# Output projections with the activations as the stationary operand, in a two-layer recurrent encoder

## The chip, the cores and the metric

The kernel runs on one core of one Trainium2 chip. The metric is the device time of one execution in microseconds (us); runs of one kernel are summed up by their median.

## What is computed

The reference is a trunk of two layers on 256 tokens of width 2048, all in float32. Each layer is a token mixer and a gated MLP, both behind an RMSNorm and both added to the residual; a last RMSNorm closes the trunk.

```python
for layer in range(2):
    hn = rmsnorm(h, norm_mix_g[layer])
    mix = mlstm_mixer(hn, ...) if layer == 0 else hgrn_mixer(hn, ...)      # each ends in  y @ w_out
    h = h + mix
    h = h + conv_glu(rmsnorm(h, norm_ffn_g[layer]), ...)                   # ends in  (gelu(c) * v) @ w_down
return rmsnorm(h, final_g)
```

The mixers are recurrences that run over the tokens in both directions: the mLSTM with 8 heads of width 256, HGRN2 with 16 heads of width 128. The MLP's hidden width is 5504, 43 tiles of 128. Four output projections add to the residual: `w_out` of the mLSTM, `w_down` of layer 0, `w_out` of HGRN2 and `w_down` of layer 1.

## The kernel before

All weights, some 440 MB, are streamed from memory once. Precision comes from a split: a float32 value is taken apart into a high part and a low part, and a product is computed from three terms, high by high, high by low and low by high. `split_weights` loads pieces of 2048 columns (`raw`, three buffers, on SP's queue), and makes two halves of 1024 columns each from it: ACT rounds `wh` out of `raw` (line 146), DVE subtracts to get `wl` (line 147), four buffers each. `stream` keeps three such halves ahead (LOOK) and issues the matmuls of a list of chunks in their order. An activation tile `x` for one k tile is 128 x 512: the 256 tokens of the high part, then the 256 of the low part.

There are two kinds of chunk. In an "fm" chunk (feature-major result) the weights are stationary and the tokens move. A chunk has 256 output features in two blocks f, and each k tile takes one pair of matmuls for each block:

```python
pe.matmul(ps[f], wh[:, c:c + P], x, start=st, stop=False)                          # line 197, 512 columns
pe.matmul(ps[f][:, 0:T], wl[:, c:c + P], x[:, 0:T], start=False, stop=sp)          # line 198, 256 columns
```

In a "tm" chunk (token-major result) a tile of `x` is stationary and 512 columns of the weights move, three matmuls for each half t of the tokens (lines 187 to 189). Before the change q, k of the mLSTM, q and both gates of HGRN2, both halves of the MLP and all output projections are fm; v and o of the mLSTM, v and g of HGRN2 are tm.

`Side` holds generators for small work, such as the heads of the mixers and the transposes of their results. `side.tick` advances a clock by an estimate of the matmul time after every k tile, and steps the generators that are due, so that their instructions land between the stream's matmuls in PE's queue. The framework orders each engine's instructions by a simulated timeline and may move them by a few places.

The residual `hx` is feature-major, 16 tiles `hT[k]` of 128 features by 256 tokens. `project` makes the chunks of an output projection: eight of them, 256 output features each. Its `done` adds the two column halves of a result to `hT[k]` (ACT copies one half to `b`, DVE adds twice, lines 310 to 312), and hands the tile to the `Norm` behind it. `Norm.add` scales the tile by the norm's weight and splits it into an `x` tile (`split`, lines 204 and 205), POOL squares it and sums the squares (lines 243 to 248), four small matmuls with a vector of ones sum over the features (L254, `pc`). `finish` takes the power -1/2 on POOL (line 280), and spreads it over the partitions by a diagonal matrix and a matmul (L286, `pr`). The scale itself is applied later, to the results of the next stage's matmuls.

The MLP runs in two parts of 22 and 21 hidden tiles: up chunks, down chunks, up chunks, down chunks. The very last chunk of the kernel has a form of its own (`last`, line 176): three matmuls of 256 columns for each k tile and block. After it the final norm is finished, DVE and POOL scale eight blocks (line 806), and eight transfers to the output follow on the queues of SP and ACT.

In the names of the trace `xt` is an x tile of a norm, `g` one of the MLP's hidden tiles, `ya` and `yb` the mixers' results, `mm` the accumulators of the stream, `pz` a transpose, `S` and `pn` matmuls of the mLSTM's heads (L426, L440), `pd` and `py` of HGRN2's (L616, L657, L658, L670), `Mb` rows of a running maximum that go through memory (`mscr`) on POOL's queue.

Of the kernel before, what the change touches and what calls it, by code (L numbers as in the profile page):

```python
# [30 lines left out]
    ("mix_g", 2 * KT), ("ffn_g", 2 * KT), ("a_head_g", KT), ("b_head_g", KT), ("final_g", KT),  # L31
# [13 lines left out]
MIX = 5  # L45
FIRST = (0, 1, 2, 4, 7, 10, 13, 16)
# [7 lines left out]
def trunk_kernel(ctx, tc, xT, pp_d, cst_d, w_first, w_aq, w_ak, w_av, w_ao, w_aout,  # L54
                 w_bq, w_bv, w_bg, w_bout, w_up, w_down, out, mscr, stop=9):
# [15 lines left out]
    hT = [hx[:, k] for k in range(KT)]  # L71
    ident = cst[:, C_ID:C_ID + P]
# [40 lines left out]
    class Chunk:  # L113
        def __init__(self, kind, src, nk, x, done, before=None, last=False):
            self.last = last
            self.kind, self.src, self.nk, self.x, self.done, self.before = kind, src, nk, x, done, before
            self.width = {"fm": 256, "tm": 512, "first": 512 + P}[kind]

    def split_weights(chunks):

        first = True
        for ch in chunks:
            total = ch.nk * ch.width
            cuts = [0]
            if ch.last and total % 1024:
                cuts.append(total % 1024)
# [24 lines left out]
    def stream(chunks):  # L151
# [10 lines left out]
        for ch in chunks:  # L162
# [4 lines left out]
            while k < ch.nk:  # L167
                fetch()
                wh, wl, n = ready.pop(0)
                if ch.last:  # L170
                    for f in range(2):
                        for kk in range(n):
                            x, c = ch.x(k + kk), kk * 256 + f * P
                            terms = ((wh, 0), (wl, 0), (wh, T))
                            for i, (w, o) in enumerate(terms):
                                pe.matmul(ps[f][:, 0:T], w[:, c:c + P], x[:, o:o + T], start=(k + kk == 0 and i == 0),  # L176
                                          stop=(k + kk == ch.nk - 1 and i == 2))
                    k += n
                    continue
                for kk in range(n):  # L180
# [13 lines left out]
                    else:  # L194
                        for f in range(len(ps)):
                            c = kk * ch.width + f * P
                            pe.matmul(ps[f], wh[:, c:c + P], x, start=st, stop=False)  # L197
                            pe.matmul(ps[f][:, 0:T], wl[:, c:c + P], x[:, 0:T], start=False, stop=sp)  # L198
                        side.tick(0.325 * len(ps))
# [23 lines left out]
    class Norm:  # L223
        def __init__(self, gname, goff, final=False, first=False):
            self.first = first
            self.g, self.o, self.final = gname, goff, final
            self.xs, self.pc = [], None

        def add(self, k):
            if self.final:  # L230
                if k % 2 == 0:
                    self.xs.append(keep.tile([P, 2, T], F32, tag=f"xt{k}", name=f"hg{k}"))
                act.activation(self.xs[k // 2][:, k % 2], hT[k], AF.Copy, scale=col(self.g, self.o + k))
            else:
                t = keep.tile([P, 2 * T], F32R, tag=f"xt{k}", name=f"xt{k}")
                split(t, hT[k], col(self.g, self.o + k))
                self.xs.append(t)
            if self.first:
                return
            eng = dve if k >= KT - 2 else pool  # L240
            if k == 0:
                self.acc = ev.tile([P, T], F32, tag="acc", bufs=2, name="acc")
                eng.tensor_tensor(self.acc, hT[k], hT[k], ALU.mult)  # L243
                return
            s = ev.tile([P, T], F32, tag="sq", bufs=2, name="sq")
            eng.tensor_tensor(s, hT[k], hT[k], ALU.mult)  # L246
            if k < KT - 2 or not self.final:
                eng.tensor_tensor(self.acc, self.acc, s, ALU.add)
                s = self.acc
            if k >= (KT - 3 if self.final else KT - 1):  # L250
                if self.pc is None:
                    self.pc = [aux("pc") for _ in range(2)]
                for t in range(2):
                    pe.matmul(self.pc[t][:, 0:1], s[:, t * P:(t + 1) * P], ones[:, 0:1],  # L254
                              start=(k == KT - 3 or not self.final), stop=(k == KT - 1))
            if k == KT - 1:
                self.finish()

        def squares(self, i, mp):
# [7 lines left out]
            if i == 3:  # L267
                a = self.acc4
                dve.tensor_tensor(a[:, 0:2 * T], a[:, 0:2 * T], a[:, 2 * T:4 * T], ALU.add)
                dve.tensor_tensor(a[:, 0:T], a[:, 0:T], a[:, T:2 * T], ALU.add)  # L270
                self.pc = [aux("pc") for _ in range(2)]
                for t in range(2):
                    pe.matmul(self.pc[t][:, 0:1], a[:, t * P:(t + 1) * P], ones[:, 0:1], start=True, stop=True)
                self.finish()

        def finish(self):
            self.rc = ev.tile([P, 2], F32, tag="rc", bufs=2, name="rc")
            for t in range(2):
                dve.tensor_scalar(self.rc[:, t:t + 1], self.pc[t][:, 0:1], 1.0 / D, EPS, ALU.mult, ALU.add)
            pool.tensor_tensor(self.rc, self.rc, hmx, ALU.pow)  # L280
            dg = ev.tile([P, T], F32, tag="sq", bufs=2, name="dg")
            for t in range(2):
                dve.tensor_scalar(dg[:, t * P:(t + 1) * P], ident, self.rc[:, t:t + 1], None, ALU.mult)
            self.pr = aux("pr")
            for t in range(2):
                pe.matmul(self.pr[:, t * P:(t + 1) * P], ones[:, 0:P], dg[:, t * P:(t + 1) * P], start=True, stop=True)  # L286
            self.R = ev.tile([P, T], F32, tag="R", bufs=2, name="R")
            act.copy(self.R, self.pr[:, 0:T])

        def x(self, k):  # L290
            return self.xs[k]

# [6 lines left out]
    def project(wsrc, nk, x, norm):  # L299

        def done(c):
            def f_(ps):
                for f in range(2):
                    k = 2 * c + f
                    if norm is not None and norm.final and c == 7:
                        dve.tensor_tensor(hT[k], hT[k], ps[f][:, 0:T], ALU.add)
                        norm.add(k)
                        continue
                    b = ev.tile([P, T], F32, tag="b", bufs=3, name="b")
                    act.copy(b, ps[f][:, T:2 * T])  # L310
                    dve.tensor_tensor(hT[k], hT[k], ps[f][:, 0:T], ALU.add)
                    dve.tensor_tensor(hT[k], hT[k], b, ALU.add)  # L312
                    if norm is not None:
                        norm.add(k)
            return f_
        return [Chunk("fm", wsrc(c), nk, x, done(c), last=(norm is not None and norm.final and c == 7))
                for c in range(8)]
# [6 lines left out]
    def mlstm(norm, nxt):  # L324
# [6 lines left out]
        def first_x(k):  # L331
            if k == len(norm.xs):
                norm.add(k)
# [86 lines left out]
        def head(st, j):  # L420
# [30 lines left out]
            for t in range(2):  # L451
                jk = ev.tile([P, T], F32, tag="jk", bufs=1, name="jk")
                act.activation(jk, y[:, t], AF.Square, accum_out=ss[:, t:t + 1])
# [22 lines left out]
        for pr in range(AH // 2):  # L476
# [34 lines left out]
            def done_first(ps, done_v=done_v):  # L511
                done_v(ps[0:2])
                gates(ps[2])

# [4 lines left out]
            chunks.append(Chunk("fm", w_aq[pr], KT, norm.x, done_q))  # L519
# [16 lines left out]
    def hgrn(norm, nxt):  # L536
# [59 lines left out]
        def head(hd):  # L596
# [75 lines left out]
            for t in range(2):  # L672
                jk = ev.tile([P, T], F32, tag="jk", bufs=1, name="jk")
# [63 lines left out]
    def ffn(layer, norm, nxt):  # L737
# [4 lines left out]
        def begin():  # L742
            box["mp"] = stack.enter_context(tc.tile_pool(name="ff", bufs=1))

# [20 lines left out]
        for part, (f0, nf) in enumerate(((0, FA), (FA, FB))):  # L765
            GT = []
            for i in range(nf):
                chunks.append(Chunk("fm", w_up[layer, f0 + i], KT, norm.x, done_up(f0 + i, i, GT),
                                    begin if f0 + i == 0 else None))
            chunks += project(lambda c: w_down[layer, c][:, f0 * 256:(f0 + nf) * 256], nf,  # L770
# [11 lines left out]
    n0, n1, n2, n3 = Norm("mix_g", 0, first=True), Norm("ffn_g", 0), Norm("mix_g", KT), Norm("ffn_g", KT)  # L782
    nf = Norm("final_g", 0, final=True)
    chunks = mlstm(n0, n1)
    if stop > 1:
        c, close0 = ffn(0, n1, n2)
        chunks += c
    if stop > 2:
        c = hgrn(n2, n3)
        b = c[0].before  # L790

        def swap():
            close0()
            b()
        c[0].before = swap
        chunks += c
    if stop > 3:
        c, close1 = ffn(1, n3, nf)
        chunks += c
    stream(chunks)  # L800
    side.drain()
    if stop > 3:
        order = ((0, pool), (2, dve), (3, dve), (1, pool), (4, dve), (5, dve), (6, dve), (7, dve))
        for n, (c, eng) in enumerate(order):
            r = (nf.R if eng is pool else nf.pr[:, 0:T]).unsqueeze(1).broadcast_to([P, 2, T])
            eng.tensor_tensor(nf.xs[c], nf.xs[c], r, ALU.mult)
            (nc.sync if n % 2 else nc.scalar).dma_start(out[c], nf.xs[c])
        close1()
    else:
        for c in range(KT // 2):  # L810
# [82 lines left out]
```

## Time and profile before

| | |
|---|---|
| median of 3 runs | 2452.22 us (2452.0 to 2452.59) |
| the profiled execution's own time | 2451.01 us |
| its span, first to last instruction | 2449.2 us |
| mean granted TensorE clock | 0.998 |
| PE busy | 2432.1 us, 99% |
| DVE busy | 1759.7 us, 72% |
| ACT busy | 1221.2 us, 50% |
| POOL busy | 267.4 us, 11% |
| weight pieces, time from issue to landing | 4.9 us for 1 MB |

Times in the profile count from the start of the span. The stages follow each other: the mLSTM's projections to 310 us, its output projection to 400, the first MLP to 1116 (down projections 645 to 767 and 1000 to 1116), HGRN2 to 1626, its output projection to 1719, the second MLP (down projections 1964 to 2086 and 2319 to 2436), the tail to 2449. The length of a matmul's record holds its way through the array, which overlaps the next matmul; the stream's rate is read from the distance between starts in the timeline. A row of the windows gives the stretch, its length, the busy time and instructions of PE, PEld, DVE, ACT and POOL, the granted clock, the share of the DMA engines and GB/s.

### The profile page before, as it was taken

What the parts mean: (1) busy time and instruction counts of PE and PEld (TensorE: products, weight loads), DVE (VectorE), ACT (ScalarE), POOL (GpSimd) and SP (SyncE); (2) the same over time, 40 slices, a digit from 0 to 9 for tenths busy, and PEclk for the clock granted to TensorE, in tenths of its full rate; (3) what the DMA queues carried; (4) which work ended last, traced back from release to release, by engine and by line L of the source; (5) the groups of instructions that cost most, each with busy time, mean ns of one, the idle gap of its engine ahead of it and who ended that gap; (6) DMA issues with size and microseconds to landing.
All of it is one profiled execution on the core that took longest, in us unless ns stands there. A gap on an engine that the chain in (4) does not pass through costs nothing.

```text
span 2449.2 us, 36986 instructions
## 1 busy us (share of the span) xinstructions
PE 2432.1 (99%) x14462; PEld 2108.3 (86%) x14462; DVE 1759.7 (72%) x2943; ACT 1221.2 (50%) x1890; POOL 267.4 (11%) x325
## 2 busy tenths in 40 slices
PE   9999999999999999999999999999999999999998
PEld 7888888888888888888888888888888888888887
DVE  7766577777656777668888888888777755677754
ACT  6655455444444444445455555545544444444443
POOL 0100032000000000122222222224000000000022
PEclk9999999999999999999999999999999999999999
DMA  7654555555556555555544445445555555555553
GB/s 261 189 179 160 184 187 184 191 191 191 179 189 202 189 189 189 181 183 191 172 160 168 162 165 172 160 156 201 186 191 191 186 189 194 189 189 189 185 190 125
DMA packets 65920, 448.88 MB, mean 183 GB/s; under 512 B 7616, under 2 KB 8256, under 8 KB 15568
## 3 DMA queue, kind: packets, MB, share of 16 engines
q1 hardware_dynamic: 63936, 443.03, 54.2%
q0 software_dynamic: 800, 2.16, 0.6%
q8 instruction: 113, 1.85, 0.3%
q10 hardware_dynamic: 1008, 1.32, 0.2%
q14 instruction: 63, 0.52, 0.1%
HBM read 444.32 MB, written 2.16 MB: 182 GB/s over the span
## 4 chain that ended last, share of the span: by engine, by line
PE 98%; DVE 1%; ACT 0%; issue 0%; DMA 0%; SPq 0%; POOL 0%; DVEq 0%; POOLq 0%
PE mm L197 53%; PE mm L198 26%; PE mm L187 5%; PE mm L189 5%; PE mm L188 5%; PE pd L616 1%; PE pn L440 1%; PE mm L176 1%; PE py L670 1%; DVE wl L147 0%; PE S L426 0%; PE pd L657 0%; DMA raw<-in_w_first 0%; DVE QK L629 0%; PE pz L691 0%
## 5 line engine op out<-in xcount | busy, mean ns | idle before, releaser
L147 DVE TENSOR_TENSOR wl<-raw,wh 128x1024 fp32r<-128x1024 f32 (+1 forms) x864 | 1047.5, 1214 | 546.4 <-ACT wh L146 533.5
L197 PE MATMUL mm<-xt,wh 128*128 128x512 f32 x3776 | 1319.5, 395 | 0.0
L146 ACT CAST wh<-raw 128x1024 fp32r<-128x1024 f32 (+1 forms) x864 | 884.1, 1025 | 833.2 <-PE mm L197 481.5
L198 PE MATMUL mm<-xt,wl 128*128 128x256 f32 x3776 | 1049.9, 278 | 0.0
L197 PEld LDWEIGHTS mm<-xt,wh 128*128 128x128 f32 x3776 | 708.3, 188 | 164.3
L198 PEld LDWEIGHTS mm<-xt,wl 128*128 128x128 f32 x3776 | 710.1, 188 | 0.8
L197 PE MATMUL mm<-g,wh 128*128 128x512 f32 x1334 | 462.6, 394 | 0.0
L198 PE MATMUL mm<-g,wl 128*128 128x256 f32 x1334 | 369.5, 277 | 0.0
L197 PEld LDWEIGHTS mm<-g,wh 128*128 128x128 f32 x1334 | 250.1, 188 | 58.0
L198 PEld LDWEIGHTS mm<-g,wl 128*128 128x128 f32 x1334 | 250.5, 188 | 0.0
L187 PE MATMUL mm<-wh,xt 128*128 128x512 f32 x512 | 201.9, 398 | 3.1 <-ACT xt L204 2.5
L188 PE MATMUL mm<-wl,xt 128*128 128x512 f32 x512 | 201.5, 394 | 0.4 <-DVE wl L147 0.4
L189 PE MATMUL mm<-wh,xt 128*128 128x512 f32 x512 | 200.6, 393 | 0.0
L209 ACT COPY b<-mm 128x256 f32<-128x256 f32 x237 | 87.6, 370 | 172.2 <-PE mm L198 172.2
L243 POOL TENSOR_TENSOR acc<-hx 128x256 f32<-128x256 f32 x4 | 4.8, 1203 | 1238.3 <-DVE hx L312 1238.3
L187 PEld LDWEIGHTS mm<-wh,xt 128*128 128x128 f32 x512 | 95.7, 188 | 23.3 <-ACT xt L204 2.7
L189 PEld LDWEIGHTS mm<-wh,xt 128*128 128x128 f32 x512 | 96.5, 188 | 19.9
L188 PEld LDWEIGHTS mm<-wl,xt 128*128 128x128 f32 x512 | 96.5, 188 | 19.4 <-DVE wl L147 0.8
L197 PE MATMUL mm<-yb,wh 128*128 128x512 f32 x256 | 89.6, 396 | 0.0
L197 PE MATMUL mm<-ya,wh 128*128 128x512 f32 x256 | 89.1, 394 | 0.0
L246 POOL TENSOR_TENSOR sq<-hx 128x256 f32<-128x256 f32 x52 | 62.7, 1214 | 193.4 <-DVE hx L312 191.2
L210 DVE TENSOR_TENSOR a<-mm,b 128x256 f32<-128x256 f32 x86 | 36.5, 425 | 50.9 <-ACT b L209 50.7
(188 smaller groups left out, 1999.2 us busy)
## 6 DMA issues: line engine op xcount, KB each, us to landing
raw<-in_w_up SPq DMA_DIRECT2D x172, 1024.0 KB, 4.9
raw<-in_w_down SPq DMA_DIRECT2D x64, 1024.0 KB, 4.8
raw<-in_w_bq SPq DMA_DIRECT2D x48, 1024.0 KB, 4.9
raw<-in_w_ao SPq DMA_DIRECT2D x16, 1024.0 KB, 4.9
raw<-in_w_aout SPq DMA_DIRECT2D x16, 1024.0 KB, 4.9
raw<-in_w_bv SPq DMA_DIRECT2D x16, 1024.0 KB, 4.9
raw<-in_w_bg SPq DMA_DIRECT2D x16, 1024.0 KB, 4.9
raw<-in_w_bout SPq DMA_DIRECT2D x16, 1024.0 KB, 4.9
```

The source lines that it names most:

```text
L146: act.copy(wh[:, :m], r)
L147: dve.tensor_tensor(wl[:, :m], r, wh[:, :m].bitcast(F32), ALU.subtract)
L176: pe.matmul(ps[f][:, 0:T], w[:, c:c + P], x[:, o:o + T], start=(k + kk == 0 and i == 0), stop=(k + kk == ch.nk - 1 and i == 2))
L187: pe.matmul(ps[t], xh, wh[:, c], start=st, stop=False)
L188: pe.matmul(ps[t], xh, wl[:, c], start=False, stop=False)
L189: pe.matmul(ps[t], xl, wh[:, c], start=False, stop=sp)
L197: pe.matmul(ps[f], wh[:, c:c + P], x, start=st, stop=False)
L198: pe.matmul(ps[f][:, 0:T], wl[:, c:c + P], x[:, 0:T], start=False, stop=sp)
L209: act.copy(b, ps[:, T:2 * T])
L210: dve.tensor_tensor(dst, ps[:, 0:T], b, ALU.add)
L246: eng.tensor_tensor(s, hT[k], hT[k], ALU.mult)
L440: pe.matmul(pn[:, 0:258], w, v, start=(i == 0), stop=(i == len(parts) - 1))
```

## The change

All output projections become tm: `project` makes four chunks of 512 output features, the weights' layout in memory changes from 256 to 512 columns, and the residual becomes token-major (`hm`, the same storage as `hx`, two halves t of 128 tokens by 2048 features). Two new loads on POOL's queue bring x in that layout behind the first chunk. `done` adds 512 columns for each t straight from PSUM.

`Norm.add` becomes a square with a sum along the row on ACT, and a generator `turn`, which transposes the residual in groups of four on PE and splits the tiles straight out of PSUM; after the last chunk it finishes the norm. `FinalNorm` takes the place of the last norm: it stays token-major, multiplies by `final_g` (loaded and spread over the partitions when the second MLP begins) and scales rows. The last chunk issues all matmuls of the remaining pieces for t = 0, then `half`, then the same for t = 1.

In an fm chunk `side.tick` moves from behind the pair to between the two matmuls of the second block's pair. Chunks have a new parameter `turns`: so many transposes of the identity into an unused accumulator, inside the second block's first pair. q chunks of the mLSTM's head pairs get 0, 1, 2 and 1, the first up chunk of each second part 1 (layer 0) and 2 (layer 1). A tile of 192 bytes (`lead`) is put ahead of the MLP's tiles. `final_g` leaves the packed parameters `pp`, which lose 64 bytes a partition.

```diff
+LEAD = 48
+    hm = hx.rearrange("p k t -> p (k t)").rearrange("p (a c) -> p a c", a=2)
...
-                if ch.last:
-                    for f in range(2):
-                        for kk in range(n):
-                            x, c = ch.x(k + kk), kk * 256 + f * P
-                            terms = ((wh, 0), (wl, 0), (wh, T))
...
+                if ch.last and k + sum(p[2] for p in ready) + n == ch.nk:
+                    pieces_, k0 = [(wh, wl, n)] + ready, k
+                    for t in range(2):
+                        k = k0
+                        for wh, wl, n in pieces_:
+                            for kk in range(n):
+                                x, c = ch.x(k), slice(kk * 512, (kk + 1) * 512)
+                                xh, xl = x[:, t * P:(t + 1) * P], x[:, T + t * P:T + (t + 1) * P]
+                                pe.matmul(ps[t], xh, wh[:, c], start=False, stop=False)
+                                pe.matmul(ps[t], xh, wl[:, c], start=False, stop=False)
+                                pe.matmul(ps[t], xl, wh[:, c], start=False, stop=k == ch.nk - 1)
+                                k += 1
+                        ch.half(ps[t], t)
+                    return
...
                             pe.matmul(ps[f], wh[:, c:c + P], x, start=st, stop=False)
+                            if f and k == 0 and ch.turns:
+                                it = aux("turns")
+                                for i in range(ch.turns):
+                                    pe.transpose(it[:, i * P:(i + 1) * P], ident, ident)
+                            if f:
+                                side.tick(0.325 * len(ps))
                             pe.matmul(ps[f][:, 0:T], wl[:, c:c + P], x[:, 0:T], start=False, stop=sp)
-                        side.tick(0.325 * len(ps))
...
+        def add(self, c):
+            if c == 0:
+                self.ss = ev.tile([P, 2, 4], F32, tag="ss8", bufs=2, name="ss8")
+            cs = slice(512 * c, 512 * c + 512)
             for t in range(2):
+                square(hm[:, t, cs], self.ss[:, t, c:c + 1])
+            side.push(self.turn(c))
+
+        def turn(self, c):
+            yield 2.5
+            for k0 in (4 * c, 4 * c + 2):
+                pz = aux("pz")
+                for k in (k0, k0 + 1):
+                    for t in range(2):
+                        o = (k - k0) * T + t * P
+                        pe.transpose(pz[:, o:o + P], hm[:, t, k * P:(k + 1) * P], ident)
+                for k in (k0, k0 + 1):
+                    self.take(k, pz[:, (k - k0) * T:(k - k0 + 1) * T])
+                yield 1.0
+            if c == 3:
...
+                self.finish([ss[:, t, 0:1] for t in range(2)])
...
+    class FinalNorm:
...
+        def half(self, ps, t):
+            side.drain()
+            cs = slice(D - 512, D)
+            h = hm[:, t, cs]
+            dve.tensor_tensor(h, h, ps, ALU.add)
+            square(h, self.ss[:, t, 3:4])
+            last = self.mp.tile([P, 512], F32, tag="fl", bufs=2, name="fl")
+            dve.tensor_tensor(last, h, self.g[:, cs], ALU.mult)
+            rc = self.rc[:, t:t + 1]
+            dve.tensor_scalar(rc, self.ss[:, t, 3:4], 1.0 / D, rc, ALU.mult, ALU.add)
+            pool.tensor_tensor(rc, rc, hmx[:, 0:1], ALU.pow)
+            for c in range(4):
+                v = last if c == 3 else hm[:, t, 512 * c:512 * c + 512]
+                if c % 2:
+                    act.activation(v, v, AF.Copy, scale=rc)
+                else:
+                    dve.tensor_scalar(v, v, rc, None, ALU.mult)
+                (nc.scalar if c % 2 else nc.sync).dma_start(out[t, :, 512 * c:512 * c + 512], v)
...
         def done(c):
             def f_(ps):
...
+                for t in range(2):
+                    h = hm[:, t, 512 * c:512 * c + 512]
+                    dve.tensor_tensor(h, h, ps[t], ALU.add)
+                if norm is not None:
+                    norm.add(c)
             return f_
...
+        chunks = [Chunk("tm", wsrc(c), nk, x, done(c)) for c in range(4)]
...
                 gates(ps[2])
+                for t in range(2):
+                    pool.dma_start(hm[:, t], x_d[t])
...
-            chunks.append(Chunk("fm", w_aq[pr], KT, norm.x, done_q))
+            chunks.append(Chunk("fm", w_aq[pr], KT, norm.x, done_q, turns=(0, 1, 2, 1)[pr]))
...
+            box["mp"].tile([P, LEAD], F32, name="lead")
+            if isinstance(nxt, FinalNorm):
+                nxt.begin(box["mp"])
...
+                                    turns=(2 if layer else 1) if part and i == 0 else 0))
```

More of the change, by code (lines that the diff above doesn't have):

```diff
@@ L113, in trunk_kernel, with __init__ @@
     class Chunk:
-        def __init__(self, kind, src, nk, x, done, before=None, last=False):
-            self.last = last
+        def __init__(self, kind, src, nk, x, done, before=None, last=False, turns=0):
+            self.last, self.turns = last, turns
             self.kind, self.src, self.nk, self.x, self.done, self.before = kind, src, nk, x, done, before
@@ L223, in trunk_kernel, with __init__, take @@
     class Norm:
[L224 to L257, printed above, removed]
+        def __init__(self, gname, goff):
+            self.g, self.o = gname, goff
+            self.xs, self.done = [None] * KT, False
+        def take(self, k, src):
+            self.xs[k] = keep.tile([P, 2 * T], F32R, tag=f"xt{k}", name=f"xt{k}")
+            split(self.xs[k], src, col(self.g, self.o + k))
         def squares(self, i, mp):
@@ L270, in squares @@
                 dve.tensor_tensor(a[:, 0:T], a[:, 0:T], a[:, T:2 * T], ALU.add)
-                self.pc = [aux("pc") for _ in range(2)]
+                pc = [aux("pc") for _ in range(2)]
                 for t in range(2):
[L273 to L277, printed above, removed]
-            for t in range(2):
-                dve.tensor_scalar(self.rc[:, t:t + 1], self.pc[t][:, 0:1], 1.0 / D, EPS, ALU.mult, ALU.add)
-            pool.tensor_tensor(self.rc, self.rc, hmx, ALU.pow)
-            dg = ev.tile([P, T], F32, tag="sq", bufs=2, name="dg")
+                    pe.matmul(pc[t][:, 0:1], a[:, t * P:(t + 1) * P], ones[:, 0:1], start=True, stop=True)
@@ L302, in f_ @@
             def f_(ps):
[L303 to L314, printed above, removed]
-            return f_
-        return [Chunk("fm", wsrc(c), nk, x, done(c), last=(norm is not None and norm.final and c == 7))
-                for c in range(8)]
+                for t in range(2):
+                    h = hm[:, t, 512 * c:512 * c + 512]
+                    dve.tensor_tensor(h, h, ps[t], ALU.add)
+                if norm is not None:
+                    norm.add(c)
+            return f_
+        chunks = [Chunk("tm", wsrc(c), nk, x, done(c)) for c in range(4)]
+        if isinstance(norm, FinalNorm):
+            chunks[3].last, chunks[3].half = True, norm.half
+        return chunks
     def slot(j, name, more=None):
@@ L513, in done_first @@
                 gates(ps[2])
+                for t in range(2):
+                    pool.dma_start(hm[:, t], x_d[t])
             if pr == 0:
@@ L781, in trunk_kernel, with swap @@
         pe.matmul(idle[:, 0:P], ones[:, 0:P], ones[:, 0:P], start=True, stop=True)
-    n0, n1, n2, n3 = Norm("mix_g", 0, first=True), Norm("ffn_g", 0), Norm("mix_g", KT), Norm("ffn_g", KT)
-    nf = Norm("final_g", 0, final=True)
+    n0, n1, n2, n3 = Norm("mix_g", 0), Norm("ffn_g", 0), Norm("mix_g", KT), Norm("ffn_g", KT)
+    nf = FinalNorm()
     chunks = mlstm(n0, n1)
[L785 to L799, printed above, removed]
-    stream(chunks)
[L801 to L810, printed above, removed]
-            nc.sync.dma_start(out[c], hx[:, 2 * c:2 * c + 2])
-        if stop == 2:
-            close0()
+    c, close0 = ffn(0, n1, n2)
+    chunks += c
+    c = hgrn(n2, n3)
+    b = c[0].before
+    def swap():
+        close0()
+        b()
+    c[0].before = swap
+    chunks += c
+    c, close1 = ffn(1, n3, nf)
+    chunks += c
+    stream(chunks)
+    close1()
 def _cols(w, width):
```

98 lines of the change are left out of this document (69 added, 29 removed).

## The prediction

> **What bounds the kernel now.** First the page: busy shares, and the chain that ended last.
>
> ```profile
> PE 2432.1 (99%) x14462; PEld 2108.3 (86%) x14462; DVE 1759.7 (72%) x2943; ACT 1221.2 (50%) x1890; POOL 267.4 (11%) x325
> ...
> PE 98%; DVE 1%; ACT 0%; issue 0%; DMA 0%; SPq 0%; POOL 0%; DVEq 0%; POOLq 0%
> ```
>
> PE is the chain from start to end. The timeline of PE shows no gap over 0.3 us in any stage but four places: the start, two of some 0.6 us at 15 to 17 us, 1.5 us at 1165 us, and the tail. So an edit is worth what it takes off PE's queue, or off the tail. Second, the windows by stage, here the first down projection and the tail after the last weight matmul:
>
> ```profile
> 644.90:766.90 122.00, 122.00 (x706) 106.70 (x705) 65.45 (x85) 52.11 (x67) 0.00 (x0) 1.00 0.57 188
> ...
> 2436.10:2449.20 13.10, 1.81 (x14) 1.46 (x12) 5.33 (x12) 0.88 (x2) 3.19 (x3) 0.69 0.43 160
> ```
>
> The clock is granted in full, DVE is busy for half of a projection. A matmul's record (395 ns) is a latency; what counts is the distance between starts. Third, the timeline of PE in three streams: fm pairs in q of head pair 1, fm pairs in an up chunk, tm matmuls in o.
>
> ```profile
> 113.26 0.40 PE L197 MATMUL mm<-xt,wh 128*128 128x512 f32 x1
> ...
> 114.32 0.40 PE L197 MATMUL mm<-xt,wh 128*128 128x512 f32 x1
> ```
> ```profile
> 524.24 0.39 PE L197 MATMUL mm<-xt,wh 128*128 128x512 f32 x1
> ...
> 525.27 0.40 PE L197 MATMUL mm<-xt,wh 128*128 128x512 f32 x1
> ```
> ```profile
> 175.37 0.39 PE L187 MATMUL mm<-wh,xt 128*128 128x512 f32 x1
> ...
> 176.05 0.39 PE L187 MATMUL mm<-wh,xt 128*128 128x512 f32 x1
> ```
>
> Each fence but the last spans three pairs: 1.06 us (353 ns a pair, "slow") and 1.03 (346.7 over long stretches, "fast"). The last spans three 512-column matmuls: 0.68 us, 226.7 each. Fm knows only these two rates: up and down chunks and output projections run fast from 324 to 1150 us and from 1664 to 2420, while q and k of mLSTM and most of HGRN are slow. A fm chunk entered from a tm chunk starts slow in nearly every case. It goes on slow until something is put between, and what that is matters: after any group of transposes or of norm matmuls (L254, L286, L468, L691) it was fast; after py or pd groups standing between pairs it stayed slow. Every group of two or four that landed inside a pair, between its wh and its wl matmul, was followed by the fast rate:
>
> ```profile
> 1269.65 0.40 PE L197 MATMUL mm<-xt,wh 128*128 128x512 f32 x1
> 1269.89 0.38 PE L691 MATMUL pz<-cst,y 128*128 128x128 f32 x2
> 1270.03 0.36 PE L198 MATMUL mm<-xt,wl 128*128 128x256 f32 x1
> 1270.23 0.40 PE L197 MATMUL mm<-xt,wh 128*128 128x512 f32 x1
> ```
>
> **The change part by part.** The profiled execution took 2451.01 us, its span is 2449.2; the median of the three runs is 2452.22, 1.2 above it. I sum against the span and carry the difference over to the median.
>
> *Projections as tm.* Removed: 1334 pairs on g, 256 on ya, 256 on yb, 1846 x 346.7 ns = 640.0 us, and the 126 L176 matmuls of the last chunk, 120 ns apart, 15.1. Added: 4 chunks x (16 + 16 + 2 x 43) k tiles = 472 steps of six 512-column matmuls, 472 x 6 x 226.7 ns = 642.0. All on PE: **-13.1**. Some 50 pairs of the two output projections now run slow: -0.3. The six new entries (the first six matmuls of a tm chunk cost some 30 ns together, the first fm pairs run slow until the first group): +0.4.
>
> *Transposes of the residual.* Each of three norms gets 32 transposes in groups of four. The nearest row is L468, the same form in a tm stream:
>
> ```profile
> 173.32 0.39 PE L189 MATMUL mm<-wh,xt 128*128 128x512 f32 x1
> 173.55 0.60 PE L468 MATMUL pz<-cst,y 128*128 128x128 f32 x4
> 173.91 0.48 PE L187 MATMUL mm<-wh,xt 128*128 128x512 f32 x1
> 174.23 0.39 PE L188 MATMUL mm<-wl,xt 128*128 128x512 f32 x1
> ```
>
> The group moves the next start by 0.36, the matmul behind it takes 0.32 instead of 0.227: 0.46 us. 24 groups: **+11.0** (+8.6 if the 0.1 behind it falls away). Four L254 groups go (0.45 each in streams, 0.4 in the last): -1.8. In one place the Trainium skill speaks against this part: its page "TensorE: Matmul & The Clock Gate", section "Part 4: PE-mode transpose", puts a transpose at about 275 ns in a kernel, bound by SBUF access. The records of L468 do last 272 ns, but their starts are 108 ns apart; by the page 96 x 275 ns would be an estimated 26 us.
>
> *Waits that the transposes bring.* PE is in order, so a group whose residual isn't added yet stops the weight stream. After a chunk's last matmul: 0.4 us to DVE's start, two adds of 512 from PSUM at 0.69 (L806's row), ready at 1.8 us; the groups come at the first tick past 2.5. DVE's weight subtraction (1.24 us) could stand ahead: then 3.1 against some 2.7. But PE lags the weights by four wh buffers, some 11 us, so it rarely does. Taken: 0; bound +0.4 x 12 chunks = +5. Behind each add in DVE's queue stand only later weight pieces, with that lead. Evacuation gets cheaper (copies and half the adds go; POOL's 1.2 us squares go), off the path: 0.
>
> *Side work and turns inside pairs.* In HGRN 530 pairs run slow, some 110 of them before the first group of a chunk. If the others turn fast: 420 x 6.6 ns = 2.8; py and pd inside a pair aren't in the trace, so bounds 0 and -2.8; taken **-2.3**, as every kind seen there turned it. The mLSTM q and k chunks of head pairs 1 to 3 (192 pairs) save 1.3. The seven added turns cost 0.13 (one) or 0.24 (two) by L691's groups: +0.9. Net -0.4. The turns at the start of each second up part keep 1344 pairs fast that now come behind a tm projection; without them +9.0.
>
> *Alignment.* By the tile sizes x and weights already agree modulo 256: pp shrinks by 64 bytes and moves both; the ev pool grows by 64 modulo 256, and the 192 bytes of lead fill that to 256 for the g tiles. No change: 0.
>
> *Loads.* x comes as two 1 MB loads on POOL's queue after mscr or, since they wait only for readers of hx that are done by 37 us, ahead of it. In the first case the Mb loads (64.2 us) stand behind up to 2 x 4.9 us of transfer; Wh is ready at 76.0, its reader pn starts at 79.2. Taken: 0; bound 9.8 - 3.2 = +6.6. The fg load stands ahead of one 0.7 us power on POOL with 8 us to spare: 0.
>
> *Tail.* Now 13.2 us from the last weight matmul's start (2435.98) to the end:
>
> ```profile
> 2436.30 0.43 DVE hx L306
> ...
> 2438.25 0.71 POOL rc L280
> ...
> 2439.33 0.72 PE pr L286 x4
> ...
> 2441.76 2.39 DVE hg L806 x4
> ```
>
> DVE ends at 2444.16, the span 5.0 later (last issues, landing, end). After: half 0 is done under half 1's 21 matmuls. For half 1: 0.43 to the add, 0.69, square 0.69 (L703's row) with its read 0.19 (L674's), rc 0.2, power 0.8, then on ACT two scalings at 0.69 with an issue of 0.54 between: 4.96, plus the same 5.0: 10.0. **-3.2**, bounds -1 and -5.
>
> Sum: -13.1 - 0.3 + 0.4 + 11.0 - 1.8 - 2.3 - 0.4 - 3.2 = -9.7. Span 2439.5, profiled time 2441.3, median 2442.5.
>
> **The rivals.**
> 1. *Turns don't turn.* A single transpose inside a pair isn't clearly in the trace (two are). If both second up parts stay slow: +9.0, 2451.5, no change.
> 2. *Slow is the rate of all fm behind tm projections* (slower). If neither turns nor norm groups hold, the 3776 pairs on xt less the 760 slow today, some 3000, turn to 353: 3000 x 6.6 ns = +19.8, and the 3.6 gained in HGRN and mLSTM is lost: 2465.9. It decides from some 1470 pairs on. Against it: L254 and L286 groups stand in today's first up chunks, and all after them is fast.
> 3. *Transposes don't overlap* (slower). At their records' 272 ns, 26.1 us in place of 11.0: 2457.6. It decides from 0.86 us a group. The 0.36 of L468 speaks against it.
> 4. *Matmuls cost columns alone.* Both forms stream 3072 columns a step, so the 13.1 vanish: 2455.6. The Trainium skill, same page, section "Back-to-back issue gap", gives N/2.4 + 2.5 ns, by which a step would fall from an estimated 1300 to 1295 ns. The starts above (1387 and 1360) don't agree.
> 5. *The change misses its alignment.* If g tiles end up off the weights, the nearest rows are the 233 ns of a tm chunk's first matmuls: 2064 x 6.3 ns = +13.0, 2455.5.
>
> **How the numbers follow.** About 0.2% (4.9 us) can be told from no change. Forecast 0.78, rivals 0.07, 0.06, 0.03, 0.02, 0.04. Faster 0.78; same 0.07 + 0.02 + 0.04 = 0.13; slower 0.09. The forecast's own bounds: down, HGRN in full, cheaper groups and the tail at -5 give 2437 or so; up, HGRN at 0, the Mb wait, or one second up part slow give 2449. With rival 1 and part of 5 the range is 2437 to 2454.
>
> **What would show it.** Down chunks of 22 k tiles at 29.9 us (now two of 15.25), 0.9 more where a norm's groups run; no L176; up chunks 11.1 us apart in both parts; 96 residual transposes with no idle time ahead; HGRN pairs at 347; PE's last matmul 10 us before the end. Wrong it is if the first up chunk behind a down projection runs at 353, if a transpose waits for DVE's add, or if pn waits for Mb.

## The result and the profile after

The changed kernel takes 2444.99 us (median of 7 runs, 2444.7 to 2446.53) against 2452.22 (2451.98 to 2452.59): a ratio of 0.9971, interval 0.996 to 0.9982, or 7.2 us off the median where 9.7 were forecast. The profiled execution took 2444.99 us with a span of 2443.2, 6.0 less than before's span; the other 1.2 are the distance of before's profiled execution from its median. The working below goes by the spans.

The page, busy shares and the chain that ended last:

```profile
PE 2431.0 (99%) x13551; PEld 2077.7 (85%) x13551; DVE 1695.7 (69%) x2784; ACT 1207.7 (49%) x1831; POOL 149.3 (6%) x219
...
PE 99%; ACT 0%; DMA 0%; issue 0%; DVE 0%; SPq 0%; POOLq 0%; POOL 0%
```

PE still is the chain. It issues 911 matmuls fewer in almost the same busy time, and POOL lost 118 us of work that was never on the path. The windows by stage, for the first down projection, HGRN2, the second up part of layer 1 and the tail:

```profile
646.20:765.90 119.70, 119.70 (x531) 99.20 (x530) 60.93 (x60) 47.51 (x48) 0.00 (x0) 1.00 0.57 192
1116.00:1623.80 507.80, 507.80 (x3514) 433.23 (x3513) 434.55 (x903) 262.46 (x477) 126.23 (x175) 1.00 0.49 167
2082.50:2320.10 237.60, 237.60 (x1347) 206.13 (x1346) 168.24 (x266) 113.99 (x165) 0.00 (x0) 1.00 0.55 187
2434.20:2443.20 9.00, 0.40 (x2) 0.00 (x0) 2.91 (x7) 3.02 (x6) 0.55 (x1) 0.80 0.62 233
```

and the same third row of before:

```profile
2085.70:2318.60 232.90, 232.90 (x1346) 203.66 (x1345) 169.35 (x269) 114.22 (x167) 0.00 (x0) 1.00 0.57 190
```

The down projection went from 122.0 to 119.7 us and the tail from 13.1 to 9.0. One stage became slower: the second up part of layer 1, 237.6 against 232.9. Taken over all stages, after less before (rounded):

| stage | us | stage | us |
|---|---|---|---|
| start | +0.5 | HGRN2 | -1.6 |
| mLSTM | -0.9 | its output projection | +0.5 |
| its output projection | +1.1 | layer 1: up, down, first part | +0.6, -2.4 |
| layer 0: up, down, first part | +0.5, -2.3 | layer 1: up, down, second part | **+4.7**, -3.4 |
| layer 0: up, down, second part | +0.1, +0.6 | tail | -4.1 |

The output projections and the second down part of layer 0 carry the transposes, so they gain nothing. The start isn't the change's: over all profiled executions the first fm chunk began between 38.4 and 40.4 us.

The timeline of PE in the first down projection, one and a half k tiles apart (nine matmuls in 2.04 us, 226.7 ns each, as in o before):

```profile
699.93 0.39 PE L191 MATMUL mm<-wh,g 128*128 128x512 f32 x1
...
701.97 0.39 PE L191 MATMUL mm<-wh,g 128*128 128x512 f32 x1
```

A group of residual transposes in the mLSTM's output projection, which has no idle time ahead of it, moves the next start by 0.35 us, and the matmul behind it takes 0.32 instead of 0.227:

```profile
361.24 0.60 PE L275 MATMUL pz<-cst,hx 128*128 128x128 f32 x4
361.59 0.48 PE L191 MATMUL mm<-wh,ya 128*128 128x512 f32 x1
361.91 0.39 PE L192 MATMUL mm<-wl,ya 128*128 128x512 f32 x1
```

The first chunk of the second up part of layer 0, and then that of layer 1, with the turns and the three pairs behind them:

```profile
766.47 0.27 PE L205 MATMUL turns<-cst 128*128 128x128 f32 x1
...
766.70 0.40 PE L201 MATMUL mm<-xt,wh 128*128 128x512 f32 x1
...
767.74 0.39 PE L201 MATMUL mm<-xt,wh 128*128 128x512 f32 x1
```
```profile
2083.07 0.38 PE L205 MATMUL turns<-cst 128*128 128x128 f32 x2
...
2083.40 0.40 PE L201 MATMUL mm<-xt,wh 128*128 128x512 f32 x1
...
2084.46 0.40 PE L201 MATMUL mm<-xt,wh 128*128 128x512 f32 x1
```

One transpose set the pairs to 1.04 us for three, two in the other place left them at 1.06, and the slow rate stayed for 668 of the 669 pairs: 668 x 6.6 ns = 4.4 us, the +4.7 of the table. The same happened behind the one turn of the mLSTM's head pair 3 (0.4 us).

The loads of x on POOL's queue, ahead of the Mb loads:

```profile
14.96 0.70 POOL L582 DMA_DIRECT2D hx<-in_x  x1 [13.69 <-ACT sq L245]
23.03 0.53 POOL L582 DMA_DIRECT2D hx<-in_x  x1 [7.36 <-ACT sq L245]
...
64.62 1.64 POOL L479 DMA_DIRECT2D Mb<-mscr  x3 [2.42 <-DMA mscr<-M]
```

They went out during the first chunk and had landed 30 us before Mb, which is issued at 64.6 as before (64.2). The tail in the timeline: last matmul, half 1's add, the power, ACT's two scalings and their transfers:

```profile
2434.21 0.39 PE L180 MATMUL mm<-wh,g 128*128 128x512 f32 x1
2434.64 0.69 DVE L346 TENSOR_TENSOR hx<-hx,mm 128x512 f32<-128x512 f32 x1
...
2436.63 0.55 POOL L352 TENSOR_TENSOR fss<-fss,mhalf 128x1 f32<-128x1 f32 x1 [2.85 <-DVE fss L351]
...
2437.22 0.72 ACT L356 ACTIVATE hx<-hx,fss 128x512 f32<-128x512 f32 x1 [0.91 <-POOL fss L352]
2437.85 0.71 ACT L356 ACTIVATE fl<-fl,fss 128x512 f32<-128x512 f32 x1
2437.97 0.34 ACTq L359 DMA_DIRECT2D out<-hx  x1
2438.58 0.34 ACTq L359 DMA_DIRECT2D out<-fl  x1
```

### The profile page after: what moved, and what is told of

The parts are those of the page before. It is cut to its first block, busy times and chain, and to the rows that moved or that the text cites. A ratio compares the mean times of both kernels' runs of the same rounds, so it can differ in the third digit from the quotient of the medians.

```text
span 2443.2 us, 34691 instructions
## 1 busy us (share of the span) xinstructions
PE 2431.0 (99%) x13551; PEld 2077.7 (85%) x13551; DVE 1695.7 (69%) x2784; ACT 1207.7 (49%) x1831; POOL 149.3 (6%) x219
## 4 chain that ended last, share of the span: by engine, by line
PE 99%; ACT 0%; DMA 0%; issue 0%; DVE 0%; SPq 0%; POOLq 0%; POOL 0%
PE mm L201 36%; PE mm L208 18%; PE mm L191 13%; PE mm L193 13%; PE mm L192 13%; PE pd L685 1%; PE pn L507 1%; PE py L739 1%; PE pz L275 0%; PE S L493 0%; PE pd L726 0%; DMA raw<-in_w_first 0%; ACT xt L213 0%; PE pd L727 0%; PE pz L760 0%
## 5 line engine op out<-in xcount | busy, mean ns | idle before, releaser
L147 DVE TENSOR_TENSOR wl<-raw,wh 128x1024 fp32r<-128x1024 f32 (+1 forms) x848 | 1031.2, 1218 | 595.2 <-ACT wh L146 586.7
L193 PE MATMUL mm<-wh,g 128*128 128x512 f32 x674 | 263.1, 390 | 0.0
L191 PE MATMUL mm<-wh,g 128*128 128x512 f32 x674 | 262.8, 390 | 0.0
L192 PE MATMUL mm<-wl,g 128*128 128x512 f32 x674 | 262.6, 390 | 0.0
L193 PEld LDWEIGHTS mm<-wh,g 128*128 128x128 f32 x674 | 126.6, 188 | 26.3
L192 PEld LDWEIGHTS mm<-wl,g 128*128 128x128 f32 x674 | 126.7, 188 | 26.1
L191 PEld LDWEIGHTS mm<-wh,g 128*128 128x128 f32 x674 | 126.7, 188 | 25.9
L704 POOL TENSOR_TENSOR G<-G 128x384 f32<-128x384 f32 (+2 forms) x96 | 65.0, 677 | 6.3
L698 DVE TENSOR_TENSOR QK<-QK,G 128x256 f32<-128x256 f32 x112 | 61.5, 549 | 0.3 <-DVE qm L677 0.3
```

The lines of the kernel that those rows point to most:

```text
L147: dve.tensor_tensor(wl[:, :m], r, wh[:, :m].bitcast(F32), ALU.subtract)
L191: pe.matmul(ps[t], xh, wh[:, c], start=st, stop=False)
L192: pe.matmul(ps[t], xh, wl[:, c], start=False, stop=False)
L193: pe.matmul(ps[t], xl, wh[:, c], start=False, stop=sp)
L698: dve.tensor_tensor(ka, ka, gview(G, n, 1, h), ALU.mult)
L704: pool.tensor_tensor(G2, G[:, 0:6 * n:2], G[:, 1:6 * n:2], ALU.mult)
```

## Experiments

The theory: the change is worth its cheaper matmuls and its shorter tail; the transposes give the first back almost whole; and what is left depends on which of two rates each fm stream falls into, which the turns decide place by place. Rivals: the rate belongs to the place and not to the turns, the transposes hide waits, the tail's gain comes from elsewhere, or the operands' addresses set the rates and the turns are a side matter. Beside these runs the kernel before took 2451.9 to 2452.1.

**Other turns.** Three sets of turns that differ from the change's in nothing else.

```diff
-    turns=(0, 1, 2, 1)[pr]))                                # q chunks of the mLSTM's head pairs
-    turns=(2 if layer else 1) if part and i == 0 else 0))   # second up parts
+    turns=(0, 2, 1, 2)[pr]))                                # swapped
+    turns=(1 if layer else 2) if part and i == 0 else 0))
+    turns=0))                                               # none, in both places
+    turns=(0, 1, 2, 2)[pr]))                                # by place
+    turns=1 if part and i == 0 else 0))
```

> Only the numbers of turns change: 0, 2, 1, 2 for the q chunks of the mLSTM (were 0, 1, 2, 1), 2 for the second up part of layer 0 (was 1) and 1 for that of layer 1 (was 2). Theory: the number of transposes at a place decides the rate of all fm pairs that follow there, so every place turns over: the second up part of layer 1 falls from 353.3 to 346.7 ns a pair (-4.5 us), that of layer 0 rises (+4.5), q and k of head pair 3 fall (-0.4), those of 1 and 2 rise (+0.8); in sum +0.4, about 2445.4. Rival: an odd number is right everywhere, or one is: then both second up parts are read off the rule (1 fast, 2 slow), the sum is the same for these, but head pair 2 goes fast and 1 and 3 slow. Second rival: the rate is a matter of the stage and not of the turns: layer 1 stays slow, layer 0 fast, 2445.0.

Swapped: 2445.07 us, ratio 0.9973 [0.9962, 0.9984].

> All turns left out. Theory: fm chunks behind tm chunks start slow and stay so: the second up part of layer 0 goes from 346.7 to 353.3 ns a pair (672 pairs, +4.5 us), that of layer 1 stays at 353.3, q and k of head pairs 1 and 2 go slow (+0.8), the turns themselves save 0.9: about +4.4, 2449.4. Rival: the turns have nothing to do with the rate: -0.9, 2444.1.

None: 2449.22 us, 0.9989 [0.9981, 0.9998]. All five places (q of the head pairs 1 to 3, and the two second up parts) ran slow from their entry on.

> Turns taken place by place from what turned the rate so far: 0, 1, 2, 2 for the q chunks of the mLSTM (head pair 3 had 1 and was slow; with 2 it was fast), 1 for the second up part of both layers (layer 1 had 2 and was slow; with 1 it was fast). Theory: which number turns a place depends on the phase in which the stream comes in, and that phase is the same as in the runs it is taken from: all five places run at 346.7 ns a pair, 670 and 62 pairs fall by 6.6 ns: -4.4 and -0.4, 2440.2. Rival: the phase depends on everything ahead, so a change at head pair 3 turns one of the later places back: 2444.6.

By place: 2440.08 us, 0.9951 [0.9938, 0.9965]. This is 4.9 us below the change and 12 below the kernel before, and the fastest version found.

The windows of PE alone show the rate as a count: in 220 us of an up stream 1271 instructions are the fast rate, 1247 the slow one. First the second up part of layer 1, then that of layer 0, with the turns swapped:

```profile
2092.00:2312.00 220.00, 220.00 (x1271) 1.00 0.57 190
772.00:992.00 220.00, 220.00 (x1247) 1.00 0.56 186
```

and with the turns by place:

```profile
2092.00:2312.00 220.00, 220.00 (x1271) 1.00 0.56 191
772.00:992.00 220.00, 220.00 (x1271) 1.00 0.57 188
```

Swapping moved the loss from layer 1 to layer 0 and left the sum where it was. So turns do turn a stream, a single one included (layer 0 is fast with one and slow with none), but in a given place one number works and the other may not. Neither "it belongs to the place" nor "every group in a pair turns it" holds.

**The tick back behind the pair.**

```diff
-                            if f:
-                                side.tick(0.325 * len(ps))
                             pe.matmul(ps[f][:, 0:T], wl[:, c:c + P], x[:, 0:T], start=False, stop=sp)
+                        side.tick(0.325 * len(ps))
```

> side.tick back behind the pair, turns kept. Theory: HGRN2's groups land behind wl matmuls again, and slow pairs rise there from 375 to some 500 of 718 (+0.9 us); norm groups do not matter; 2445.9. Rival: groups between pairs always stay slow, so first up chunks and first q chunks of HGRN2 stay slow to the end of their parts (3 x 670 pairs, +13 us): 2458.

It took 2444.57 us, 0.997 [0.9959, 0.9982], as the change did. In HGRN2 382 pairs ran slow, and 375 with the tick inside: the place of the tick is worth nothing. But with the same turns in the same places the second up part of layer 0 was now slow (654 of the 655 pairs in a stretch of 232 us) and that of layer 1 fast. The other kernels agree; turns, and F for the fast rate, S for the slow one:

| kernel | head pair 1 | 2 | 3 | up 2, layer 0 | up 2, layer 1 |
|---|---|---|---|---|---|
| the change | 1 F | 2 F | 1 S | 1 F | 2 S |
| swapped | 2 F | 1 S | 2 F | 2 S | 1 F |
| tick behind | 1 F | 2 F | 1 S | 1 S | 2 F |
| by place | 1 F | 2 F | 2 F | 1 F | 1 F |
| double transposes | 1 F | 2 F | 1 S | 1 S | 2 F |
| no lead | 1 F | 2 F | 1 S | 1 S | 2 F |
| last chunk whole | 1 F | 2 F | 1 S | 1 F | 2 S |
| 256 bytes | 1 F | 2 F | 1 S | 1 F | 2 S |

The head pairs answer alike in every row. The up parts do not: their number also depends on what ran ahead. Each row is read from one profiled execution, and as two exchanged up parts cancel in the time, the other executions can't confirm those rows; that all five places can be fast at once is borne out by all five executions with turns by place, within 0.4 us of each other.

What exactly a turn shifts remains open. In layer 0 the entry, from the 512-column matmul ahead of the turn to the turn, was 235 ns in the change and 237 with the tick behind, but it doesn't decide: without the lead it was 235 too, and there one turn left the part slow.

**Double transposes.** Each of the 96 residual transposes is issued twice, to the same place.

```diff
-                        pe.transpose(pz[:, o:o + P], hm[:, t, k * P:(k + 1) * P], ident)
+                        for _ in range(2):
+                            pe.transpose(pz[:, o:o + P], hm[:, t, k * P:(k + 1) * P], ident)
```

> Every transpose of the residual is issued twice into the same place, 96 more of them. Theory: a transpose costs its distance of starts on PE, 0.109 us, and nothing waits: +10.5 us, 2455.5, with the norm's matmuls and all x tiles in time. Rival 1: they overlap the stream's matmuls as their neighbours' records do: +2 or less. Rival 2: they cost their records' 272 ns: +26, 2471. Apart from that a second up part that changes its rate moves any of these by 4.5.

It took 2455.92 us, 1.0017 [1.0008, 1.0026]: 10.9 more than the change. The two up parts changed places (+4.5, -4.5) and cancel. Stage by stage the 96 transposes account for 10.5, 0.109 us each, as expected; the other 0.4 are some 60 more slow pairs in HGRN2's first fm chunks. The record of one such transpose lasts 272 ns, and the Trainium skill ("TensorE: Matmul & The Clock Gate", "Part 4: PE-mode transpose") gives some 275 ns in a kernel; as a price in this stream, 0.109 decides.

**The last chunk whole.** It is issued like the other tm chunks, and both halves are finished after it.

```diff
-            chunks[3].last, chunks[3].half = True, norm.half
+            half = norm.half
+            chunks[3].done = lambda ps: [half(ps[t], t) for t in range(2)]
```

> The last chunk is issued like the others, k tile by k tile for both halves of the tokens, and both halves are finished after it. Theory: half 0's chain (3.2 us on DVE, from its add at 2431.5 to the last scaling at 2434.7 in the changed kernel) no longer lies beside half 1's matmuls and stands in DVE's queue ahead of half 1's add: +2.5 to +3.2, 2448. Rival: the two chains interleave on ACT, POOL and DVE, and the transfers at the end set the time: +0 to +1, 2445.5.

It took 2447.71 us, 0.9983 [0.9974, 0.9992], 2.7 more than the change. The amount is as expected, the way only in part. The two halves' chains interleave on DVE and ACT, so ACT ends only 1.05 us later (2439.60 against 2438.55), and the rest comes from the transfers: from ACT's last scaling to the end it takes 6.2 us instead of 4.65, with all eight issued close together.

**Addresses.** A tile of 64, 128 or 256 bytes is put ahead of the weights' buffers, which moves them against the x tiles. By the tile sizes the distance between them is 0 modulo 256 in the change.

```diff
+    wpool.tile([P, 16], F32, name="off")      # 64 bytes; 32: 128 bytes; 64: 256 bytes
```

> A tile of 64 bytes ahead of the weight buffers moves weights (and the 22 g tiles that lie outside the first 16 slots) by 64 bytes against all x tiles in the first 16 slots; nothing else is changed. Theory: the alignment of x and weights modulo 256 sets the rate: fm pairs go to 353 ns or more on nearly all 3776 pairs (about 1050 are slow already: +18 us), and tm steps get slower than 226.7 ns a matmul too, by the 6 ns of their first matmuls at most (4368 matmuls, up to +26): 2463 to 2489. Rival: the alignment does nothing; the time stays within 5 us, as modes of single stretches may change: 2440 to 2450.

64 bytes: 2468.15 us, 1.0068 [1.0056, 1.0081], 23.2 over the change.

> The same with 128 bytes: weights 128 bytes off the first 16 x tiles modulo 256, aligned modulo 128. Theory: the period is 256, so tm steps are slower than with 64 bytes or between 2.3 and 6.8 ns a matmul (the two distances measured so far), 3840 matmuls, +9 to +26, and fm pairs run at 353 or more: 2465 to 2490. Rival: the period is 128 or less, 2445.

128 bytes: 2472.77 us, 1.0085 [1.0071, 1.0099], 27.8 over it.

> The control of the run with 64 bytes: a tile of 256 bytes ahead of the weight buffers, so that everything behind moves and x and weights still agree modulo 256. Theory: only the distance modulo 256 counts, and the time is that of the changed kernel, 2445.0 (4.5 more or less if a second up part changes its rate). Rival: any distance, or the buffers' own places, made the 23 us: some 2468.

256 bytes: 2445.03 us, 0.997 [0.9959, 0.9982], the same as the change. The windows of the wh matmuls in the first up part of layer 0 (PE, then PEld), with 64, 128 and 256 bytes:

```profile
416.00:640.00 224.00, 223.93 (x635) 119.06 (x634) 1.00 0.56 185
```
```profile
416.00:640.00 224.00, 223.93 (x640) 119.75 (x639) 1.00 0.57 188
```
```profile
416.00:640.00 224.00, 224.00 (x648) 121.18 (x647) 1.00 0.57 190
```

The distance modulo 256 between the stationary and the moving operand sets the rate: 64 bytes off, fm pairs take 353 ns behind turns and norm groups too, and tm matmuls some 229; at 128 bytes 351 and 231 to 233. That it is the distance, and not the weights' own place, shows inside the run with 64 bytes: the last 6 or 5 hidden tiles of each part lie behind the weights and moved with them, and there the matmuls stay at 226.7. Nine matmuls in the first down projection, on tiles that stayed and on tiles that moved along:

```profile
670.46 0.39 PE L192 MATMUL mm<-wh,g 128*128 128x512 f32 x1
...
672.52 0.39 PE L192 MATMUL mm<-wh,g 128*128 128x512 f32 x1
...
680.05 0.39 PE L192 MATMUL mm<-wh,g 128*128 128x512 f32 x1
...
682.09 0.39 PE L192 MATMUL mm<-wh,g 128*128 128x512 f32 x1
```

With 64 bytes some 2500 pairs turn slow (2500 x 6.6 ns = 16.5 us) and the 3840 tm matmuls on tiles that stayed lose 1.7 ns each on average (6.6 us), together the 23.2 within 0.1. The Trainium skill ("SBUF — State Buffer", "Operand start alignment") allows any start that is a multiple of the element and says that its runs timed nothing; these did, and the start has a price.

**No lead.** The 192 bytes ahead of the MLP's tiles are left out.

```diff
-            box["mp"].tile([P, LEAD], F32, name="lead")
```

> The 192 bytes of lead ahead of the MLP's tiles are left out, so that the g tiles 16 and up (22 of 86) lie 64 bytes off the weights modulo 256; all others stay aligned. Theory: by the run with 64 bytes, a tm matmul on a tile that is off takes 229.0 ns instead of 226.7, so 22 k tiles x 4 chunks x 6 matmuls = 528 x 2.3 ns = +1.2 us, seen in the down chunks alone; 2446.2. Rival, as the prediction had it: the alignment of all g tiles hangs on the lead and costs 6.3 ns on 2064 matmuls: +13, 2458. Apart from that a second up part may change its rate (4.5).

It took 2448.68 us, 0.9986 [0.9978, 0.9995], 3.7 more. Only 22 of the 86 hidden tiles, 528 matmuls, lie behind the lead (the first 16 of each part are elsewhere); modulo 256 they moved by 64 bytes, the other way than in the run with 64 bytes. On them the stream alternates between 236 and 231 ns; nine matmuls in the down projection:

```profile
668.70 0.39 PE L191 MATMUL mm<-wh,g 128*128 128x512 f32 x1
...
670.79 0.40 PE L191 MATMUL mm<-wh,g 128*128 128x512 f32 x1
```

2.09 us, 233 each, for 226.7: 528 x 6.7 ns = 3.5. The same distance costs three times as much in one direction as in the other, which the expectation had taken as equal.

## Why the prediction was right, and where it fell short

**Projections as tm** (-13.1): right where it stands alone. A first down part has 88 k steps in four chunks, each 26.6 ns cheaper (1386.8 to 1360.2): -2.34; measured -2.3 and -2.4. That the busy time of 512-column matmuls can be traded against pairs by their starts, and not by their records or columns, is what carried this; rival 4 would have left these two stages as they were.

**Transposes** (+11.0): a group of four that stands alone in a tm stream costs 0.44 us by the starts. The framework broke most groups up, but each eight cost 0.90 to 0.93 all the same, 11.0 in all; doubling them cost 10.5. Rival 3 (272 ns each) falls. No transpose waited for an add, as taken.

**Turns** (second up parts at 0): here the prediction failed. The step was "Every group of two or four that landed inside a pair, between its wh and its wl matmul, was followed by the fast rate", and from it that "the turns at the start of each second up part keep 1344 pairs fast". Half of rival 1 came true, for the wrong reason: it doubted the single transpose, and it was the two that didn't turn. Its own sign of being wrong, a first up chunk behind a down projection at 353, came in layer 1. The rows of before held only transposes that had happened to fit, and the prediction lists no group that turns a fast stream slow; yet in the same trace the pd groups at 1255.83 us, between two pairs, turn a fast stream slow (1.04 us for three pairs ahead of them, 1.06 behind), as they do in two more places:

```profile
1254.35 0.39 PE L197 MATMUL mm<-xt,wh 128*128 128x512 f32 x1
...
1255.39 0.39 PE L197 MATMUL mm<-xt,wh 128*128 128x512 f32 x1
...
1255.83 1.15 PE L616 MATMUL pd<-qm,km 128*64 128x64 f32 x32
...
1258.16 0.40 PE L197 MATMUL mm<-xt,wh 128*128 128x512 f32 x1
...
1259.22 0.40 PE L197 MATMUL mm<-xt,wh 128*128 128x512 f32 x1
```

That the median still came within 2.5 us of the forecast, with 4.5 lost here, is in part luck: 1.9 more than the sum has were gained in the tail and in what isn't traced below, and the profiled execution of before lies 1.2 under its median, while that of the change lies on it. With the places that failed set to the other number, the forecast's -9.7 is exceeded: 12 us under before.

**HGRN2** (-2.3): -1.6, by other means. The slow pairs went from 501 (the prediction has 530) to 375, not to 110: -0.8. "As every kind seen there turned it" was wrong: what a group does hangs on its place and not on its kind. A head's pd groups, 36 matmuls inside one pair, left the pairs behind them at 353 in four places and turned them fast in three. The first place of each sort, with three pairs behind:

```profile
1190.46 1.15 PE L685 MATMUL pd<-qm,km 128*64 128x64 f32 x32
...
1192.21 0.39 PE L201 MATMUL mm<-xt,wh 128*128 128x512 f32 x1
...
1193.27 0.40 PE L201 MATMUL mm<-xt,wh 128*128 128x512 f32 x1
```
```profile
1254.45 1.15 PE L685 MATMUL pd<-qm,km 128*64 128x64 f32 x32
...
1256.56 0.39 PE L201 MATMUL mm<-xt,wh 128*128 128x512 f32 x1
...
1257.60 0.39 PE L201 MATMUL mm<-xt,wh 128*128 128x512 f32 x1
```

Two pz inside a pair at 1249.18 us leave the stream slow, and two between pairs at 1268.21 turn it from fast to slow, each in three places; in before both pairs of transposes stood inside a pair and were followed by the fast rate. The tick inside gave none of the gain, as the run with the tick behind the pair showed (382 slow pairs). The gain comes from four py groups, the first at some 1197 us, which turn the stream fast with the tick in either place and leave it slow in before; why remains open. What the prediction had not counted is the 1.5 us stall at 1165 us, which is gone: PE is busy for all 507.80 us of the window, where before 1.2 were idle. With the 0.8 that makes 2.0; the 0.4 that are missing aren't traced.

**mLSTM** (192 pairs at -1.3, less 0.5 for its three groups of turns, so -0.8): -0.9, although head pair 3 is still slow, which costs 0.4.

**Tail** (-3.2): -4.2, from the last matmul's start to the end 9.0 instead of 10.0. The terms that were too large are the power (0.55 for 0.8), the two scalings on ACT (1.34 from the first's start to the second's end for 1.92, as the second starts at 2437.85, ahead of the first's transfer at 2437.97) and the way from there to the end (4.65 for 5.0); gaps between the steps, which the sum had left out, take 0.2 back. The sum's own terms add up to 4.92, not 4.96, which changes nothing. Without the split last chunk 2.7 of it are lost.

**Alignment, loads, waits** (0): as taken. Rival 5's price, 6.3 ns a matmul, was close to the 6.7 of the run without lead, but its reach was counted too large: 528 matmuls hang on the lead, not 2064. The loads of x took the earlier of the two courses, so the Mb bound of +6.6 never came into play.

From the sum of -9.7 to the span's -6.0: +4.5 second up part of layer 1, +0.7 HGRN2, -0.1 mLSTM, -1.0 tail, +0.5 start, and -0.9 that isn't traced further.

## What to carry to other kernels

On a stream bound by matmuls, count the distance between starts for each form of step, and price every inserted instruction as the shift of the next starts; both held here to 0.2 us, the steps over a stage of 120 us and the transposes over all 96. A rate that depends on how a stream is entered isn't a property that can be inferred from the cases in one trace: count it for each stream after every edit, also where the edit is elsewhere, since moving the side work changed which of two streams, with their turns untouched, was the fast one. And for float32 matmuls like these, put the stationary and the moving operand at the same address modulo 256 bytes before anything else is tuned: losing that cost 23 to 28 us here, the whole change gained 7.

## What the runs showed of the hardware

- fm pairs (512 and 256 columns, float32 rounded, stationary weights) have two stable rates, 346.7 and 353.3 ns; a stream keeps the one that it falls into for 668 pairs. One or two transposes inside a pair, or a group of other matmuls inside or between pairs, can change it, to the fast rate or to the slow one; the same group did so in some places and not in others.
- The stationary and the moving operand at the same address modulo 256 bytes: 226.7 ns for 512 columns. 64 bytes off one way some 229, the other way 233; 128 bytes 231 to 233; 256 bytes as 0.
- A float32 transpose of 128 x 128 lasts 272 ns by its record and costs 0.11 us in the stream.
